# Feed-forwards of a two-block network: two tiles of each later set as plain products instead of seven products of summed quarters

## The chip, the cores and the metric

The kernel runs on one core of one Trainium2 chip, as a single program. The metric is device time in microseconds of one execution. Before the change the median of three runs is 1578.16 us, between 1577.29 and 1581.78 us.

## The reference, cut to what matters

All is float32, with 512 tokens and a model width of 1024. A first network has two layers: a pooling mixer and a feed-forward, then latent attention and a feed-forward. A second network of one layer follows, with differential attention and a mixture of experts. Only the two feed-forwards of the first network are touched by the change:

```python
def swiglu(h, w_gate, w_up, w_down):
    return (jax.nn.silu(h @ w_gate) * (h @ w_up)) @ w_down

h = rms_norm(x, norm_ffn[i])
x = x + swiglu(h, ffn_w_gate[i], ffn_w_up[i], ffn_w_down[i])
```

The gate and the up matrix are 1024 by 2816 each, the down matrix is 2816 by 1024.

## The kernel before, in words

**Three matmuls for one product.** TensorE multiplies in a float32 form that drops low bits, so each operand is split into a high and a low part: ScalarE (ACT) writes the high part as a rounded copy, and VectorE (DVE) or GpSimd (POOL) subtracts it from the original to get the low part. A product is then three matmuls: high by high, high by low, low by high (`mm3`). The weights come from memory in float32, so all of them are split while the kernel runs.

**Tiles and sets.** The hidden width of 2816 is cut into 22 tiles of 128 columns. `SETS` makes three sets of 8, 7 and 7 tiles. For each set the kernel first computes its gate and up tiles one by one (`ffn`, the loop over `j`), and then the set's share of the down product, for 8 blocks of 128 outputs (the loop over `d`), which is added to `x`. One tile's gate and up weights are one chunk of 128 by 2048, 1024 KB.

**Plain tile.** `plain` (tiles 0 to 4) and `later` (tile 5, on the normed x that `mixed_x` leaves in `full`) multiply a whole chunk: gate and up, each over 8 pieces of the width, 3 matmuls each, so 48 matmuls of 512 columns in two PSUM banks. `later` then does one silu, one product with the up bank and the split of the hidden tile (`hidden`). The chunk is split in four parts of 512 columns by `split_part`: four copies by ACT, two subtractions by DVE and two by POOL (`POOLED`).

**Mixed tile.** `mixed` (tiles 6 to 21) takes the chunk as a 2 by 2 grid of quarters (gate and up, by even and odd pieces of the width) and x as a 2 by 2 grid (even and odd pieces, by halves of the tokens), and forms the four result quarters from seven products of summed quarters instead of eight. That is 7 x 4 x 3 = 84 matmuls of 256 columns, in four PSUM banks. The sums of the weight quarters, their splits and the sums of the products are extra elementwise work: `split_mixed` is a list of eight steps (0 to 7), which leaves a first group of weights for products 0 to 3 (ready with step 5) and a second for products 4 to 6 (steps 6 and 7: one ACT copy of 1536 columns, then one DVE subtraction of 1536). Counted in the code, a mixed tile has 15 DVE instructions and a `later` tile 4.

**What sets the order.** The order of all instructions is written out by the program. `Stream.pump` takes the weight stream one step on and is called at fixed places: after each of the 7 products of a mixed tile and once more, and 16 times in `later`. The stream holds 2 raw chunks and 3 pairs of split chunks (`BUFS`). A plain chunk takes one pair, a mixed chunk two. `room` refuses a step while no pair is free; a pair is given back by `release` behind its last product. A raw buffer is loaded anew when its chunk's last step has been issued. `extra` holds table work for the layer that follows (for layer 0 the rotation tables, DVE and ACT work): one step behind product 3 and one behind product 6 of each mixed tile. All elementwise instructions are issued by one helper, so the profile puts them on one line, L445, and they are told apart by their tiles: `raw`, `hi`, `lo` are the weights, `bh`, `bl` the parts of x, `t`, `u` the result quarters, `hh`, `hl` the hidden tile, `rs` the sum of two weight quarters.

Of the kernel before, what the change touches and what calls it, by code (L numbers as in the profile page):

```python
# [22 lines left out]
FF = 2816  # L23
FT = FF // P

SETS = ((0, 8), (8, 15), (15, 22))
PLAIN = 6
H = T // 2


# [532 lines left out]
class Net:  # L563
# [296 lines left out]
    def mixed_x(self, l, full, parts):  # L860
# [3 lines left out]
        dve = nc.vector  # L864
        a, b = slice(0, H), slice(H, T)

# [43 lines left out]
    def ffn(self, l, hooks, after, extra=None):  # L910
# [13 lines left out]
        def go(n=1):  # L924

            for _ in range(n):
                if tail and next(tail[0], True):
                    tail.pop(0)

        def rest():  # L930
            while tail:
                go()

        def hidden(t):
            hh.append(self.tmp("hh", F32R))
            hl.append(self.tmp("hl", F32R))
            h, r = hh[-1], hl[-1]
            nc.scalar.activation(h, t, AF.Copy)
            yield
            nc.vector.tensor_tensor(r, t, h.bitcast(F32), op=OP.subtract)  # L940
# [10 lines left out]
        def plain(j):  # L951
            wh, wl = self.ws.take()
            pp = []

            def mm(m, k, begin, end):
                o = (2 * m + k % 2) * T + k // 2 * P
                c = slice(o, o + P)
                self.mm3(pp[m], wh[:, c], wl[:, c], xh[k], xl[k], begin, end)

            if j == PLAIN - 2:  # L960
                pp += [self.acc(), self.acc()]
                for k in range(KT):
                    for m in range(2):
                        mm(m, k, k == 0, k == KT - 1)
                    xh[k] = xl[k] = None
                    if k < 2:
                        go()
                    if k > 1:
                        next(mix, None)
                    if k == 4:  # L970
                        self.ws.pump(4)
            else:
                for m in range(2):
                    pp.append(self.acc())
                    for n, k in enumerate((0, 2, 4, 6, 1, 3, 5, 7)):
                        mm(m, k, n == 0, n == KT - 1)
                        if n in (0, 2):
                            go()
                        if not hooks and n in (1, 3, 6):
                            next(mix, None)  # L980
                    self.ws.pump(3)
                    if hooks:
                        hooks.pop(0)()
            self.ws.release()
            pend.append(pp)
            if not hooks:
                while pend:
                    tail.append(evac(*pend.pop(0)))
                    go()

        def later():
            wh, wl = self.ws.take()
            pp = []
            for m in range(2):
                ps = self.acc()
                for n, k in enumerate((0, 2, 4, 6, 1, 3, 5, 7)):
                    o = (2 * m + k % 2) * T + k // 2 * P
                    c = slice(o, o + P)
                    self.mm3(ps, wh[:, c], wl[:, c], *full[k], n == 0, n == KT - 1)
                    go()  # L1000
                    self.ws.pump()
                pp.append(ps)
            self.ws.release()
            t = self.tmp("t")
            nc.scalar.activation(t, pp[0], AF.Silu)
            nc.vector.tensor_tensor(t, t, pp[1], op=OP.mult)
            tail.append(hidden(t))
            go()

        def mixed():  # L1010
            g, s = self.tmp("t"), self.tmp("u")
            g0, g1, s0, s1 = g[:, :H], g[:, H:], s[:, :H], s[:, H:]
            got = None

            def product(n, out):
                nonlocal got
                if n in (0, 4):
                    got = self.ws.take_group(n == 4)
                c = (n % 4) * T
                for i, (bh, bl) in enumerate(parts[n]):  # L1020
                    k = slice(c + i * P, c + (i + 1) * P)
                    self.mm3(out, got[0][:, k], got[1][:, k], bh, bl, i == 0, i == KT // 2 - 1)
                if n in (3, 6):
                    self.ws.release()
                    if extra:
                        next(extra, None)
                go()
                self.ws.pump()

            def add(dst, x, y):  # L1030
                nc.vector.tensor_tensor(dst, x, y, op=OP.add)

            bank = []
            for n in range(7):
                if n % 2 == 0:
                    ps = self.acc()
                    bank += [ps[:, :H], ps[:, H:]]
                product(n, bank[n])
                if n == 1:
                    nc.scalar.activation(s1, bank[0], AF.Copy)  # L1040
                    add(g0, s1, bank[1])
                elif n == 3:
                    add(s0, s1, bank[2])
                    add(g1, s0, bank[3])
                    self.ws.pump()
                elif n == 5:
                    add(s1, g1, bank[5])
                    add(g1, g1, bank[4])
                    add(s0, s0, bank[5])
                    nc.scalar.activation(g, g, AF.Silu)  # L1050
            add(s0, s0, bank[6])
            nc.vector.tensor_tensor(g, g, s, op=OP.mult)
            tail.append(hidden(g))
            go()

        for f0, f1 in SETS:
            hh.clear()
            hl.clear()
            for j in range(f0, f1):
                if j < PLAIN - 1:  # L1060
                    plain(j)
                elif j < PLAIN:
                    for _ in mix:
                        pass
                    later()
                else:
                    mixed()
            rest()
            for d in range(KT):
                wh, wl = self.ws.take()  # L1070
                ps = self.acc()
                n = f1 - f0
                for f in range(n):
                    c = slice(f * P, (f + 1) * P)
                    self.mm3(ps, wh[:, c], wl[:, c], hh[f], hl[f], f == 0, f == n - 1)
                    if f % 3 == 1:
                        self.ws.pump()
                self.ws.flush()
                self.ws.release()
                nc.vector.tensor_tensor(self.x[:, d], ps, self.x[:, d], op=OP.add)  # L1080
                if f1 == FT:
                    after(d)

    def plain(self, j):
        return j < PLAIN

    def ffn_weights(self, l, arena=0):
        for f0, f1 in SETS:
            for j in range(f0, f1):
                self.ws.add(self.a["ffn_gu"][l, j], j < arena, not self.plain(j))  # L1090
            for d in range(KT):
                self.ws.add(self.a["ffn_dn"][l, d, :, f0 * P:f1 * P])
# [1409 lines left out]
```

## Time and profile before

| | us |
|---|---|
| median of three runs | 1578.16 |
| the profiled execution, its own time | 1573.54 |
| span of that execution, first to last instruction | 1571.7 |
| TensorE (PE) busy | 1494.9 |
| VectorE (DVE) busy | 1142.3 |
| ScalarE (ACT) busy | 827.7 |
| GpSimd (POOL) busy | 409.8 |

The span is what the trace shows of the profiled execution; 1.8 us of its time lie around it. PE counts as busy while any of its overlapping matmuls runs, so a matmul's own duration is longer than its share of the time: what it costs in a stream is read from the distance of two starts. A PE wait appears as idle time before the matmul that waited, with the engine that ended it. "PEclk" is the granted TensorE clock as a share of full speed.

### The profile page before, as it was taken

Reading aid. Unit: us, or ns where it says so; the run is one execution under the profiler, and the core shown is the slowest. Engines: PE = TensorE matmul, PEld = TensorE weight load, DVE = VectorE, ACT = ScalarE, POOL = GpSimd, SP = SyncE. Lnnn points to the kernel's source line nnn. Section 1 sums busy time; section 2 is a strip of 40 time slices with the busy share of each in tenths; the row PEclk is TensorE's granted clock in tenths of the full one; section 3 lists DMA queues with packets and bytes.
Section 4 is the critical chain, followed back from the end, with each engine's and each line's share of the span. In section 5 each row is a group of like instructions: output and inputs, shape, how many; then the busy total and the mean of one; then the engine's idle time right before and its main releaser. Section 6 shows DMA issues by size and latency. Waiting matters only on the chain.

```text
span 1571.7 us, 24066 instructions
## 1 busy us (share of the span) xinstructions
PE 1494.9 (95%) x8849; PEld 1263.2 (80%) x8849; DVE 1142.3 (73%) x2036; ACT 827.7 (53%) x1617; POOL 409.8 (26%) x330
## 2 busy tenths in 40 slices
PE   8999989989999999999999999999979799999997
PEld 7888878888878887888889889999978666666664
DVE  6794786686577756955965876898887487878774
ACT  5442343334455644433433444777785277777774
POOL 3323221231341112232222223223212223222221
PEclk9999999999999999999999999999989899999999
DMA  6114223323411103142222223121128799999982
GB/s 213 72 57 125 77 81 95 108 81 85 142 63 46 50 1 134 63 139 85 104 83 96 104 80 122 55 81 54 68 72 302 242 306 354 367 361 372 368 306 31
DMA packets 72250, 221.76 MB, mean 141 GB/s; under 512 B 7873, under 2 KB 17217, under 8 KB 58945
## 3 DMA queue, kind: packets, MB, share of 16 engines
q1 hardware_dynamic: 58752, 201.03, 36.8%
q0 software_dynamic: 4064, 14.16, 3.9%
q10 hardware_dynamic: 9312, 5.01, 1.1%
q8 instruction: 70, 1.15, 0.3%
q14 instruction: 52, 0.42, 0.1%
HBM read 208.63 MB, written 11.53 MB: 140 GB/s over the span
## 4 chain that ended last, share of the span: by engine, by line
PE 66%; DVE 18%; ACT 7%; issue 5%; DMA 3%; POOL 1%; ACTq 0%; DVEq 0%; POOLq 0%; SPq 0%
PE acc L445 54%; PE pss L445 8%; DVE lo L445 5%; PE pst L445 4%; DVE t L445 4%; ACT hi L445 3%; DVE u L445 2%; DVE raw L445 2%; DVE p L445 1%; DVE bl L445 1%; DMA raw<-ffn_gu 1%; DVE x L445 1%; DVE xl L445 1%; ACT p L445 1%; DMA bnd<-bands 0%
## 5 line engine op out<-in xcount | busy, mean ns | idle before, releaser
L445 ACT ACTIVATE hi<-raw 128x512 fp32r<-128x512 f32 (+3 forms) x346 | 242.8, 728 | 233.3 <-DVE raw L445 107.6
L445 PE MATMUL acc<-bh,lo 128*128 128x256 f32 (+1 forms) x928 | 271.4, 292 | 23.5 <-DVE lo L445 23.5
L445 DVE TENSOR_TENSOR lo<-raw,hi 128x512 fp32r<-128x512 f32 (+2 forms) x237 | 254.2, 1074 | 37.2 <-ACT hi L445 37.1
L445 PE MATMUL acc<-bh,hi 128*128 128x256 f32 (+1 forms) x928 | 269.7, 291 | 3.4 <-ACT hi L445 3.4
L445 PE MATMUL acc<-bl,hi 128*128 128x256 f32 (+1 forms) x928 | 268.6, 289 | 0.0
L445 POOL TENSOR_TENSOR lo<-raw,hi 128x512 fp32r<-128x512 f32 (+2 forms) x109 | 142.5, 1309 | 474.7 <-ACT hi L445 408.7
L445 DVE TENSOR_TENSOR wl<-raw,wh 128x512 fp32r<-128x512 f32 x288 | 202.6, 747 | 53.0 <-ACT wh L445 43.0
L445 PEld LDWEIGHTS acc<-bh,lo 128*128 128x128 f32 x928 | 180.7, 195 | 30.0 <-DVE lo L445 28.8
L445 PEld LDWEIGHTS acc<-bh,hi 128*128 128x128 f32 x928 | 180.6, 195 | 6.7 <-ACT hi L445 5.2
L445 PEld LDWEIGHTS acc<-bl,hi 128*128 128x128 f32 x928 | 180.8, 195 | 1.6
L445 ACT ACTIVATE wh<-raw 128x512 fp32r<-128x512 f32 x320 | 177.4, 620 | 0.0
L445 DVE TENSOR_TENSOR x<-acc,x 128x512 f32<-128x512 f32 x75 | 51.4, 688 | 121.6 <-PE acc L445 121.5
L445 PE MATMUL acc<-hl,hi 128*128 128x512 f32 x352 | 137.5, 391 | 0.2 <-DVE hl L445 0.2
L445 PE MATMUL acc<-hh,hi 128*128 128x512 f32 x352 | 137.2, 390 | 0.3 <-ACT hh L445 0.3
L445 PE MATMUL acc<-hh,lo 128*128 128x512 f32 x352 | 137.0, 389 | 0.0
L445 PE MATMUL acc<-hi,xh 128*128 128x256 f32 x384 | 111.0, 289 | 0.0
L445 PE MATMUL acc<-lo,xh 128*128 128x256 f32 x384 | 108.7, 283 | 0.6 <-DVE lo L445 0.6
L445 PE MATMUL acc<-hi,xl 128*128 128x256 f32 x384 | 108.5, 283 | 0.0
L445 PE MATMUL acc<-wh,teh 128*96 128x512 f32 x224 | 103.1, 460 | 0.0
L445 POOL TENSOR_TENSOR rs<-raw 128x512 f32<-128x512 f32 x32 | 45.2, 1412 | 218.7 <-DVE u L445 74.0
L445 PE MATMUL acc<-wl,teh 128*96 128x512 f32 x224 | 88.1, 393 | 0.8 <-DVE wl L445 0.8
L445 PE MATMUL acc<-wh,tel 128*96 128x512 f32 x224 | 88.5, 395 | 0.0
(349 smaller groups left out, 3446.5 us busy)
## 6 DMA issues: line engine op xcount, KB each, us to landing
raw<-moe_w SPq DMA_DIRECT2D x200, 256.0 KB
raw<-moe_w SPq DMA_DIRECT2D x46, 1024.0 KB
raw<-ffn_gu SPq DMA_DIRECT2D x43, 1024.0 KB
raw<-ffn_dn SPq DMA_DIRECT2D x32, 448.0 KB
raw<-da_in SPq DMA_DIRECT2D x12, 1024.0 KB
raw<-ffn_dn SPq DMA_DIRECT2D x16, 512.0 KB
raw<-mla_up SPq DMA_DIRECT2D x4, 832.0 KB
raw<-mla_o_a SPq DMA_DIRECT2D x12, 256.0 KB
```

Of the source, the lines that this page charges most:

```text
L445: r = f(*args, **kw)
```

## The change

`plain` also answers yes for the second and the fifth tile (offsets 1 and 4) of the second and the third set, in both layers. These tiles (9, 12, 16 and 19) are no longer marked as mixed in the weight stream, and the loop calls `later` for them. A set of seven then runs M P M M P M M (M mixed, P plain), and 12 of 22 tiles are mixed instead of 16.

```diff
+BETWEEN = (1, 4)
...
                     for _ in mix:
                         pass
                     later()
+                elif self.plain(j):
+                    later()
                 else:
                     mixed()
...
     def plain(self, j):
-        return j < PLAIN
+        return j < PLAIN or any(f0 and j - f0 in BETWEEN for f0, f1 in SETS if f0 <= j < f1)
```

In the list of instructions, eight tiles change in all (two layers, two sets, two tiles): 36 matmuls, 11 DVE instructions and 1 ACT instruction fewer for each. The order of every engine is the same outside these four stretches, and so is the order of the loads.

The first place is ACT in the third set of layer 0, where the second group of a mixed tile that follows another mixed tile is copied. Before, for the set's second tile (the first two rows are the silu and the hidden copy of the tile ahead):

```order
L445 ACTIVATE t<-t 128x512
L445 ACTIVATE hh<-t 128x512
L445 ACTIVATE hi<-raw 128x1536
L445 ACTIVATE u<-acc 128x256
L445 ACTIVATE hi<-raw 128x1024
L445 ACTIVATE hi<-rs 128x512
```

Now, for the set's fourth tile, which follows the third (the last row but two is the third tile's silu):

```order
L447 ACTIVATE hi<-rs 128x512
L447 ACTIVATE hi<-raw 128x512
L447 ACTIVATE hi<-raw 128x1536
L447 ACTIVATE t<-t 128x512
L447 ACTIVATE hh<-t 128x512
L447 ACTIVATE hi<-raw 128x512 x2
```

The copy of 1536 columns has moved ahead of the silu and the hidden copy of the tile before it; the rows of 512 behind are parts of the next, plain chunk.

The second place is DVE at the same two tiles. Before:

```order
L445 TENSOR_TENSOR u<-u,acc 128x256
L445 TENSOR_TENSOR t<-t,u 128x512
L445 TENSOR_TENSOR hl<-t,hh 128x512
L445 TENSOR_TENSOR lo<-raw,hi 128x1536
L445 TENSOR_TENSOR t<-u,acc 128x256
L445 TENSOR_TENSOR lo<-raw,hi 128x1024
```

Now:

```order
L447 TENSOR_TENSOR u<-t,acc 128x256
L447 TENSOR_TENSOR t<-t,acc 128x256
L447 TENSOR_TENSOR u<-u,acc 128x256
L447 TENSOR_TENSOR lo<-raw,hi 128x1536
L447 TENSOR_TENSOR u<-u,acc 128x256
L447 TENSOR_TENSOR t<-t,u 128x512
L447 TENSOR_TENSOR hl<-t,hh 128x512
L447 TENSOR_TENSOR lo<-raw,hi 128x512
```

The subtraction of 1536 columns stood behind the whole tail of the tile ahead (last sum, product with silu, split of the hidden tile); now it stands in front of that tail.

## Rows read from the trace of the kernel before

**Rows 1.** The page: span, PE and DVE, and the chain that ended last.

```profile
span 1571.7 us, 24066 instructions
...
PE 1494.9 (95%) x8849; PEld 1263.2 (80%) x8849; DVE 1142.3 (73%) x2036; ACT 827.7 (53%) x1617; POOL 409.8 (26%) x330
...
PE 66%; DVE 18%; ACT 7%; issue 5%; DMA 3%; POOL 1%; ACTq 0%; DVEq 0%; POOLq 0%; SPq 0%
```

**Rows 2.** Busy time by stretch: gate and up of sets 2, 3, both layers.

```profile
core 0: us, PE busy (x) PEld busy (x) DVE busy (x) ACT busy (x) POOL busy (x), PEclk, DMA share, GB/s
169.18:253.77 84.59, 75.14 (x590) 72.70 (x588) 71.50 (x106) 33.23 (x49) 15.84 (x11) 0.98 0.23 77
292.09:372.49 80.40, 74.08 (x590) 72.46 (x588) 67.41 (x99) 33.56 (x48) 16.54 (x11) 0.98 0.24 81
728.60:808.18 79.58, 73.83 (x589) 72.40 (x588) 66.69 (x97) 32.38 (x47) 16.49 (x11) 0.98 0.25 83
846.29:925.81 79.52, 74.10 (x590) 72.48 (x588) 67.32 (x99) 33.71 (x48) 16.88 (x11) 0.98 0.24 81
sum 324.09, PE 297.16 PEld 290.04 DVE 272.92 ACT 132.88 POOL 65.74; mean PE 74.29 PEld 72.51 DVE 68.23 ACT 33.22 POOL 16.44
```

**Rows 3.** Start and duration on PE: a plain tile's end, a mixed tile's start.

```profile
105.03 0.39 PE L445 MATMUL acc<-bl,hi 128*128 128x512 f32 x1
105.26 0.39 PE L445 MATMUL acc<-bh,lo 128*128 128x512 f32 x1
105.48 0.28 PE L445 MATMUL acc<-bh,hi 128*128 128x256 f32 x1
105.60 0.28 PE L445 MATMUL acc<-bl,hi 128*128 128x256 f32 x1
```

**Rows 4.** Busy time by stretch, set 1: plain tile 5, mixed 6, 7; both layers.

```profile
94.60:105.48 10.88, 10.88 (x49) 9.01 (x48) 10.35 (x16) 3.96 (x7) 2.49 (x4) 1.00 0.08 26
105.48:125.64 20.16, 20.16 (x170) 20.15 (x169) 17.65 (x29) 9.41 (x16) 2.64 (x2) 1.00 0.27 79
652.84:663.76 10.92, 10.92 (x50) 8.96 (x49) 10.37 (x17) 5.06 (x9) 1.39 (x2) 1.00 0.09 24
663.76:683.91 20.15, 20.15 (x170) 20.15 (x168) 16.05 (x28) 9.62 (x15) 5.50 (x15) 1.00 0.36 110
```

**Rows 5.** PE by form, third set, layer 0: busy, mean ns, idle before, releaser.

```profile
L445 PE MATMUL acc<-bh,lo 128*128 128x256 f32 x196 | 56.7, 289 | 5.4 <-DVE lo L445 5.4
```

**Rows 6.** Busy time by stretch: inside the second set of layer 0.

```profile
226.48:229.89 3.41, 3.41 (x17) 3.41 (x17) 3.38 (x7) 0.82 (x2) 0.00 (x0) 0.50 0.77 262
```

**Rows 7.** In order of time, third set of layer 0, second tile: ACT.

```profile
305.45 0.63 ACT L445 ACTIVATE hh<-t 128x512 fp32r<-128x512 f32 x1 [2.97 <-DVE t L445]
305.99 1.47 ACT L445 ACTIVATE hi<-raw 128x1536 fp32r<-128x1536 f32 x1
```

**Rows 8.** The same tile: DVE, then PE.

```profile
304.15 1.27 DVE L445 TENSOR_TENSOR t<-t,u 128x512 f32<-128x512 f32 x1
307.49 1.76 DVE L445 TENSOR_TENSOR lo<-raw,hi 128x1536 fp32r<-128x1536 f32 x1 [0.68 <-ACT hi L445]
...
309.31 0.39 PE L445 MATMUL acc<-bh,lo 128*128 128x256 f32 x1 [0.98 <-DVE lo L445]
```

**Rows 9.** DVE by form, 94.60 to 125.64: a plain tile's DVE work.

```profile
L445 DVE TENSOR_TENSOR lo<-raw,hi 128x512 fp32r<-128x512 f32 x4 | 3.3, 834 | 0.0
L445 DVE TENSOR_TENSOR hl<-t,hh 128x512 fp32r<-128x512 f32 x3 | 2.1, 693 | 1.5 <-ACT hh L445 1.5
L445 DVE TENSOR_TENSOR t<-t,acc 128x512 f32<-128x512 f32 x1 | 0.7, 681 | 0.0
```

**Rows 10.** In order of time, set 1 of layer 0, tile 7's second group: DVE.

```profile
116.32 1.75 DVE L445 TENSOR_TENSOR lo<-raw,hi 128x1536 fp32r<-128x1536 f32 x1
```

**Rows 11.** DVE by form, second set of layer 0: a step of the tables.

```profile
L445 DVE SCALAR_TENSOR_TENSOR ang<-k,ang 128x512 f32<-128x512 f32 x4 | 3.2, 808 | 0.0
```

**Rows 12.** Who waited for whom, third set of layer 0: total, times, longest.

```profile
POOL rs L445 <- DMA raw<-ffn_gu: 9.5, 1, 9.5
```

## The prediction

> **What bounds the kernel now.** I read the page first, then the busy times of the stretches that the change touches, then single instructions in them. The page says that PE is busy for 1494.9 us of 1571.7, that most of the chain that ended last is PE's (66%), and that DVE has the next share (18%) [rows 1]. So two things can shorten the kernel: fewer or cheaper matmuls, or fewer waits of PE for DVE. The change makes the matmuls dearer, so all depends on the waits.
>
> The four touched stretches are the gate and up products of sets 2 and 3 in both layers. They take 84.59, 80.40, 79.58 and 79.52 us, together 324.09 [rows 2]. What they would take without a wait follows from the distance of two starts: a matmul of 256 columns follows another after 0.12 us (105.48 to 105.60), one of 512 after 0.22 to 0.23 (105.03, 105.26, 105.48) [rows 3]. A mixed tile has 84 of the first kind: 84 x 0.12 = 10.08 us. The two mixed tiles of set 1 take just that: 20.16 and 20.15 us, with PE busy throughout [rows 4]. Seven tiles should then take 70.56, and four stretches 4 x 70.56 = 282.2. The difference, 324.1 - 282.2 = **41.9 us**, is lost to waiting, 1.5 us for each of 28 mixed tiles.
>
> Where it goes: PE's idle time in the four stretches is 324.09 - 297.16 = 26.9 us [rows 2]. In the third set of layer 0 nearly all of it, 5.4 us, is ended by DVE writing `lo` [rows 5]. The granted clock is 0.98 in each stretch [rows 2], where it is 1.00 in set 1 [rows 4]; in one piece of 3.41 us after a series of waits it is 0.50, the 1.2 GHz level [rows 6]. Half of such a piece is lost, 1.7 us, so four of them make about 6.8. The remaining 8 us are the slow restarts: the matmul behind a wait takes 0.39 us instead of 0.28 [rows 3, 8], and the next one starts late.
>
> Why DVE is late: one wait followed back. In the third set's second tile, DVE's product with silu runs from 304.15 to 305.42 [rows 8], ACT's hidden copy follows to 306.08, and only behind it stands the copy of 1536 columns, from 305.99 to 307.46 [rows 7]. Then DVE subtracts, 307.49 to 309.25, and PE, which waited 0.98 us for this, starts at 309.31 [rows 8]. So the second group of a tile's weights is made behind the tail of the tile before it. DVE has no time to catch up: it is busy 67.41 us for seven tiles, 9.6 us a tile, against PE's 10.08, and in the second set of layer 0, which carries the table steps, 71.50, 10.2 us a tile [rows 2].
>
> **The change part by part.** *Matmuls.* In each stretch two mixed tiles go, 2 x 10.08 us of PE time, and two plain ones come. A plain tile took 10.88 and 10.92 us in set 1, with PE busy throughout [rows 4]; I take 10.90. Each swap costs 10.90 - 10.08 = 0.82 us on the path, eight cost **+6.6 us**. This part is certain, since PE runs it in any case.
>
> On this price a rule speaks more strongly against the change. By the Trainium skill, TensorE: Matmul & The Clock Gate, section "Wait — 56ns, not 53.3ns?", back-to-back matmuls start N / 2.4 GHz plus about 2.5 ns apart at the full clock, which an estimate makes 109 ns for 256 columns and 216 for 512. By it a swap would cost 48 x 0.216 - 84 x 0.109 = 1.2 us, eight 9.7, and the forecast would be 3 us later. The trace does not agree: it shows 120 ns and 227 (10.90 / 48), so the short matmuls carry more of the fixed cost here than the page has.
>
> *Elementwise work.* A mixed tile's 15 DVE instructions become 4. The four cost 2 x 0.834 for `lo`, 0.681 for the product with the up bank and 0.693 for `hl`, in sum 3.0 us [rows 9]. A stretch then asks DVE for 5 x 9.6 + 2 x 3.0 = 54 us while PE runs 5 x 10.08 + 2 x 10.90 = 72.2. In the second set of layer 0 ten table steps fall into the stretch; at 0.808 us [rows 11] they bring it to 62. In the third set of layer 0 DVE's share goes from 67.41 of 80.40 (84%) to 75%; in the second it is 86% of a stretch without waits. ACT and POOL were busy at most 33.71 and 16.88 us of some 80 [rows 2] and stay far below. That work lies beside PE and costs nothing as long as it comes in time, which the order decides:
>
> *Order.* `later` calls the stream 16 times and needs only two PSUM banks and one pair of split chunks. The mixed chunk behind a plain tile is finished during it, and the stream comes a full tile ahead. The eight steps of the mixed tile after that then fit into the eight calls of the first one, so that its copy and its subtraction of 1536 columns now stand ahead of the first tile's tail and no longer behind it; the two listings of the change show this on ACT and DVE. Whether this is early enough is shown by set 1, where the same three tiles P M M already run in this order. There tile 7's subtraction of 1536 columns ends at 116.32 + 1.75 = 118.07 [rows 10]. Tile 7 starts at 105.48 + 10.08 = 115.56 and needs it for its fifth product, 48 matmuls later, at 121.3: 3.2 us to spare. In the second set of layer 0 two table steps of 0.8 us lie ahead instead of a shorter one, so at least 1.6 us are left.
>
> *Waits that stay.* The trace has no set M P M M P M M, so I bound them. Below, nothing: set 1 has no PE idle time in P M M in either layer [rows 4]. Above, each of the 20 mixed tiles left keeps its 1.5 us: 20 x 1.5 = 29.9. I take zero, since set 1 has the same code in the same order; the first tile of a set, which follows the down products, has no wait now either (in the third set of layer 0 the first is the second tile's at 309.31 [rows 8]).
>
> *Edits at no cost.* The order of the loads is unchanged. A mixed chunk behind a plain one is loaded when the tile before that has emptied its buffer; POOL once waited 9.5 us for a load [rows 12]. The plain tile's 10.9 us cover it. The last table step of layer 0 moves into the third set; 0.8 us of DVE, hidden. The down products and all else keep their order.
>
> **Sum.** 20 x 10.08 + 8 x 10.90 = 201.6 + 87.2 = 288.8 us instead of 324.1: **35.3 us less**. The profiled execution would go from 1573.54 to 1538.2. That execution was 4.6 us faster than the median of the runs shown, 1578.16; against the median the forecast is **1542.9 us**.
>
> **The rivals.** *The second mixed tile of each pair still waits.* It has no plain tile ahead of it, its first group gets its pair only when the plain tile ends, and DVE has 9.6 us of work in its 10.08. Eight such tiles at 1.5 us keep 12 us: 1542.9 + 12.0 = 1554.9. Against it stands the margin of 3.2 us in set 1.
>
> *Waits per mixed tile stay as they are*, because they come from the tile's own chain of ACT, DVE and PSUM and not from lack of DVE time: 29.9 us stay, 5.4 are gained, 1572.8. For it: the wait is ended by DVE at moments when DVE itself has waited, 0.68 us for ACT [rows 8]. Against it: set 1 has the same chain without a wait.
>
> *Slower: the load comes too late at a plain tile.* With two raw buffers the chunk behind a plain tile cannot be loaded before the mixed tile ahead has used its own; ACT's first copy of it stands in the queue ahead of that tile's silu, so a late load would hold back ACT, then DVE, then PE. If the whole 9.5 us of the one such wait [rows 12] reached PE at each of eight plain tiles, that would be 76 us: 1542.9 + 76.0 = 1618.9. It decides from 35.3 / 8 = 4.4 us a tile on. Against it: the wait ended inside a tile's time and fell on POOL, and a whole plain tile lies between the load and its use.
>
> That the change does not do what it says is excluded by the listing of instructions.
>
> **How the numbers follow.** The forecast gets 0.72, the rival of the pair 0.14, unchanged waits 0.08, the late load 0.03; 0.03 is left for a result near the old time for a reason I do not see. A measurement of this kernel can tell about 0.3% from no change, 4.7 us. Forecast, pair and most of the unchanged waits (1572.8 is 5.4 below) are faster by more: 0.92. Within 0.3%: 0.05. Slower: 0.03. The range takes in the forecast and the pair rival. Its low end is 4.6 us under the forecast, as the profiled execution was under its median: 1538. Its high end is the pair rival plus 3.6 us, the distance of the slowest run shown from the median: 1559.
>
> **What would show it.** Right: the four stretches at 72 to 73 us each with PE idle near zero, plain tiles of 10.9, granted clock 1.00, DVE below 65 us in each. The pair rival would show idle time ended by `lo` in the fourth and the seventh tile of each set and nowhere else. The late load would show ACT waiting for `raw` from memory and PE waiting in the tile behind. A saving that appears outside the four stretches, or waits for `lo` right after a plain tile, would make the reasoning wrong even if the time came out.

## Result and profile after

The changed kernel takes 1539.39 us, median of four runs (1534.21 to 1539.75), against 1577.72 for the kernel before in the same comparison: a ratio of 0.9746, 95% interval 0.9718 to 0.9774. The traced execution took 1539.18 us. Two later comparisons gave medians of 1537.99 (ratio 0.975, interval 0.9725 to 0.9774) and 1542.22 (0.9763, interval 0.9740 to 0.9786).

The page of the changed kernel, which answers to [rows 1]:

```profile
span 1537.4 us, 23426 instructions
...
PE 1487.6 (97%) x8561; PEld 1250.4 (81%) x8561; DVE 1088.1 (71%) x1948; ACT 815.8 (53%) x1609; POOL 414.0 (27%) x330
...
PE 82%; DVE 7%; ACT 5%; DMA 2%; issue 1%; POOL 1%; ACTq 0%; POOLq 0%; SPq 0%; DVEq 0%
```

PE's part of the chain rose from 66% to 82%, DVE's fell from 18% to 7%. Busy times by stretch, for the same four stretches as [rows 2]:

```profile
168.87:241.06 72.19, 72.19 (x517) 68.40 (x516) 58.23 (x86) 30.54 (x47) 21.06 (x14) 1.00 0.29 94
279.17:351.36 72.19, 72.19 (x517) 68.40 (x516) 57.17 (x81) 31.16 (x47) 21.16 (x14) 1.00 0.29 94
706.60:778.79 72.19, 72.19 (x518) 68.40 (x516) 54.05 (x78) 30.03 (x46) 20.41 (x14) 1.00 0.29 94
816.90:889.09 72.19, 72.19 (x518) 68.40 (x516) 55.63 (x80) 31.26 (x47) 21.83 (x14) 1.00 0.28 94
sum 288.76, PE 288.76 PEld 273.60 DVE 225.08 ACT 123.00 POOL 84.45; mean PE 72.19 PEld 68.40 DVE 56.27 ACT 30.75 POOL 21.11
```

PE is busy for all of the 72.19 us, four times over, and the granted clock is 1.00 instead of 0.98. The sum went from 324.09 to 288.76. One of the new plain tiles, the second tile of the first of these stretches:

```profile
178.94:189.85 10.91, 10.91 (x50) 9.02 (x49) 9.07 (x10) 4.06 (x6) 4.17 (x3) 1.00 0.19 81
```

In the third set of layer 0 the matmuls that had waited 5.4 us for `lo` [rows 5] wait no more (PE by form, idle time behind the second bar):

```profile
L447 PE MATMUL acc<-bh,lo 128*128 128x256 f32 x140 | 39.6, 283 | 0.0
```

And in order of time on DVE, the subtraction of 1536 columns for that set's fourth tile, which answers to [rows 10]:

```profile
310.11 1.75 DVE L447 TENSOR_TENSOR lo<-raw,hi 128x1536 fp32r<-128x1536 f32 x1
```

The third tile starts at 279.17 + 10.08 + 10.90 = 300.15, the fourth 10.08 us later at 310.23, and its fifth product, which needs this, is due 48 matmuls (5.76 us) later, at 316.0. It is ready at 311.86, 4.1 us early.

### The profile page after: what moved, and what is told of

Read it like the earlier page. It is cut to its first block, busy times and chain, and to the rows that moved or that the text cites. A ratio compares the mean times of both kernels' runs of the same rounds, so it can differ in the third digit from the quotient of the medians.

```text
span 1537.4 us, 23426 instructions
## 1 busy us (share of the span) xinstructions
PE 1487.6 (97%) x8561; PEld 1250.4 (81%) x8561; DVE 1088.1 (71%) x1948; ACT 815.8 (53%) x1609; POOL 414.0 (27%) x330
## 4 chain that ended last, share of the span: by engine, by line
PE 82%; DVE 7%; ACT 5%; DMA 2%; issue 1%; POOL 1%; ACTq 0%; POOLq 0%; SPq 0%; DVEq 0%
PE acc L447 70%; PE pss L447 8%; PE pst L447 4%; DVE lo L447 1%; DVE bl L447 1%; ACT hi L447 1%; ACT p L447 1%; DMA raw<-ffn_gu 1%; DVE xl L447 1%; DMA bnd<-bands 1%; DVE t L447 1%; DVE p L447 1%; DVE x L447 0%; DMA out<-ring,idx 0%; DVE xe L447 0%
## 5 line engine op out<-in xcount | busy, mean ns | idle before, releaser
L447 ACT ACTIVATE hi<-raw 128x512 fp32r<-128x512 f32 (+3 forms) x354 | 235.7, 697 | 211.2 <-PE acc L447 95.8
L447 POOL TENSOR_TENSOR lo<-raw,hi 128x512 fp32r<-128x512 f32 (+2 forms) x125 | 167.0, 1340 | 629.7 <-ACT hi L447 600.4
L447 PE MATMUL acc<-bl,hi 128*128 128x256 f32 (+1 forms) x832 | 252.5, 304 | 0.0
L447 PE MATMUL acc<-bh,hi 128*128 128x256 f32 (+1 forms) x832 | 252.5, 303 | 0.0
L447 PE MATMUL acc<-bh,lo 128*128 128x256 f32 (+1 forms) x832 | 252.4, 303 | 0.0
L447 DVE TENSOR_TENSOR lo<-raw,hi 128x512 fp32r<-128x512 f32 (+2 forms) x229 | 230.9, 1010 | 28.5 <-ACT hi L447 28.0
L447 PEld LDWEIGHTS acc<-bl,hi 128*128 128x128 f32 x832 | 159.0, 191 | 6.6
L447 PEld LDWEIGHTS acc<-bh,hi 128*128 128x128 f32 x832 | 159.0, 191 | 6.6
L447 PEld LDWEIGHTS acc<-bh,lo 128*128 128x128 f32 x832 | 159.0, 191 | 6.3
L447 PE MATMUL acc<-xh,hi 128*128 128x512 f32 x200 | 79.8, 399 | 1.2 <-ACT xh L447 1.2
```

Source lines behind the costliest of these rows:

```text
L447: r = f(*args, **kw)
```

## Experiments

What is open is why the waits are gone: because the order put the second weight group ahead of the previous tile's tail, or because DVE has less to do. Each diff is against the changed kernel unless it says otherwise.

**The order without the relief.** No plain tile in between; at the end of the down products the stream is taken as far ahead as it goes:

```diff
-BETWEEN = (1, 4)
+BETWEEN = ()
...
                     if f % 3 == 1:
                         self.ws.pump()
+                if d >= 6 and f1 < FT:
+                    self.ws.pump(8)
                 self.ws.flush()
```

> No plain tile at offsets 1 and 4 (16 of 22 tiles mixed, as before), but the weight stream is taken as far ahead as its buffers allow at the end of the down products of sets 1 and 2, so that in sets 2 and 3 each copy and subtraction of 1536 columns stands ahead of the tail of the tile before it. Theory of the order (PE waited because the second weight group was made behind the previous tile's tail; DVE itself, 9.6 us a tile against 10.08, can keep up): the four stretches take 7 x 10.08 = 70.6 us each, 282 in sum, no waits for lo, and the kernel takes 1539.4 - 6.6 = 1533 us. Theory of the load on DVE (PE waited because DVE has too much work in a mixed tile, and the 88 instructions fewer removed the waits): the first two tiles go through, then the waits come back at up to 1.5 us a tile, stretches of 77 to 80 us, 1560 to 1572 us.

Measured: 1556.37 us, ratio 0.9855 (0.9830 to 0.9880). The four stretches:

```profile
169.28:247.31 78.03, 74.67 (x590) 72.62 (x589) 69.92 (x105) 33.39 (x49) 17.28 (x11) 0.98 0.23 80
286.36:359.77 73.41, 71.44 (x589) 70.80 (x588) 64.80 (x97) 32.77 (x47) 17.04 (x11) 1.00 0.25 85
716.01:788.95 72.94, 71.47 (x589) 70.81 (x588) 64.44 (x95) 32.07 (x45) 17.89 (x11) 1.00 0.25 85
828.71:902.99 74.28, 71.46 (x590) 70.81 (x589) 65.58 (x96) 31.94 (x45) 16.62 (x11) 1.00 0.25 84
sum 298.66, PE 289.04 PEld 285.04 DVE 264.73 ACT 130.17 POOL 68.83; mean PE 72.26 PEld 71.26 DVE 66.18 ACT 32.54 POOL 17.21
```

The lead is worth 25 us of the 41.9 (324.09 - 298.66), but not all. In the third set of layer 0 no wait comes for 44 us, then one of 0.73 us and one of 1.23; the second set of layer 0 waits from 34 us on. DVE falls behind, tile by tile. Its timeline in the fifth and the sixth tile of that third set:

```profile
331.67 1.75 DVE L447 TENSOR_TENSOR lo<-raw,hi 128x1536 fp32r<-128x1536 f32 x1
...
335.25 0.69 DVE L447 TENSOR_TENSOR hl<-t,hh 128x512 fp32r<-128x512 f32 x1 [0.70 <-ACT hh L447]
336.19 1.23 DVE L447 TENSOR_TENSOR lo<-raw,hi 128x1024 fp32r<-128x1024 f32 x1 [0.26 <-ACT hi L447]
...
339.66 1.00 DVE L447 TENSOR_TENSOR raw<-raw 128x512 f32<-128x512 f32 x1
340.58 1.76 DVE L447 TENSOR_TENSOR lo<-raw,hi 128x512 fp32r<-128x512 f32 x1
...
343.38 1.75 DVE L447 TENSOR_TENSOR lo<-raw,hi 128x1536 fp32r<-128x1536 f32 x1
```

And POOL's at the time of two slow instructions, those at 339.66 and 340.58:

```profile
338.52 1.59 POOL L447 TENSOR_TENSOR rs<-raw 128x512 f32<-128x512 f32 x1 [8.44 <-DMA raw<-ffn_gu]
340.19 1.61 POOL L447 TENSOR_TENSOR raw<-raw 128x512 f32<-128x512 f32 x1
```

From one subtraction of 1536 columns to the next DVE needs 343.38 - 331.67 = 11.71 us, PE 10.08. DVE is idle for only 0.96 of it, both times for ACT. Two instructions that take 0.68 us in the run without POOL's sums below take 1.00 and 1.76 while POOL works. The two waits of PE in this set:

```profile
330.69 0.39 PE L447 MATMUL acc<-bh,lo 128*128 128x256 f32 x1 [0.73 <-DVE lo L447]
342.40 0.39 PE L447 MATMUL acc<-bh,lo 128*128 128x256 f32 x1 [1.23 <-DVE lo L447]
```

The second is ended by the slow subtraction of 512 columns itself (340.58 + 1.76 = 342.34), the first by the same instruction one tile earlier, and not by the subtraction of 1536. So DVE's load is the deeper bound, and the order only puts off the moment when it shows.

**The relief without the order.** The plain tiles stay, but take the stream only four steps on, so that the subtraction of 1536 columns stands behind the tail of the tile before it again:

```diff
                     go()
-                    self.ws.pump()
+                    if j == PLAIN - 1 or n % 4 == 3:
+                        self.ws.pump()
                 pp.append(ps)
```

> The changed kernel with its plain tiles at offsets 1 and 4, but they take the weight stream only 4 steps on instead of up to 16, so that the next tiles' copy and subtraction of 1536 columns stand behind the tail of the tile before them, as before the change. DVE has the same work as in the changed kernel. Theory of the order: waits for lo come back at the fifth product of the mixed tiles at offsets 2, 3, 5 and 6, about 1.4 us each, some 5.6 us a stretch: 77 to 78 us, about 1561 us. Theory of the load on DVE: no waits, 72.2 us a stretch, 1539 us.

Measured: 1544.56 us in one run, and in the four stretches:

```profile
168.97:242.52 73.55, 72.70 (x518) 68.51 (x516) 57.51 (x83) 29.44 (x46) 19.83 (x13) 1.00 0.26 89
280.85:353.04 72.19, 72.19 (x518) 68.40 (x516) 55.88 (x77) 29.45 (x44) 20.70 (x13) 1.00 0.27 92
708.81:781.00 72.19, 72.19 (x517) 68.39 (x516) 53.27 (x75) 29.26 (x45) 20.03 (x13) 1.00 0.28 91
819.14:891.33 72.19, 72.19 (x517) 68.40 (x516) 54.93 (x77) 30.50 (x46) 21.50 (x14) 1.00 0.27 92
```

The theory that the new order is needed falls: with the old order three stretches have no wait, and the one with the table steps loses 1.4 us. The rest of this one execution's distance from the changed kernel lies mostly behind 929 us, where it takes 613.36 us at a granted clock of 0.96; the change does nothing there. It is close, though. In the third set of layer 0:

```profile
314.30 0.69 DVE L447 TENSOR_TENSOR hl<-t,hh 128x512 fp32r<-128x512 f32 x1 [0.70 <-ACT hh L447]
315.67 1.76 DVE L447 TENSOR_TENSOR lo<-raw,hi 128x1536 fp32r<-128x1536 f32 x1 [0.68 <-ACT hi L447]
```

The fourth tile starts at 280.85 + 2 x 10.08 + 10.90 = 311.9 and needs this at 317.7; it is there at 317.43, 0.2 us early, against 4.1 in the changed kernel. With the plain tiles in place, what the order adds is margin.

**One plain tile instead of two.**

```diff
-BETWEEN = (1, 4)
+BETWEEN = (1,)
```

> One plain tile a set instead of two, the second (offset 1): M P M M M M M. Theory of the order: the stream is a tile ahead behind the plain tile and stays there, no waits, 6 x 10.08 + 10.90 = 71.4 us a stretch, 285.5 in sum, 1536 us. Theory of the load on DVE: no waits up to the fourth tile, then 1.5 us in each of the last three or four, 76 to 77 us a stretch, about 1558 us.

Measured: 1545.66 us, ratio 0.9803 (0.9777 to 0.9829). Sum of the four stretches, and then the four groups of down products behind them:

```profile
sum 288.65, PE 287.06 PEld 278.28 DVE 247.23 ACT 127.93 POOL 81.13; mean PE 71.76 PEld 69.57 DVE 61.81 ACT 31.98 POOL 20.28
...
sum 155.94, PE 154.38 PEld 125.87 DVE 81.30 ACT 59.24 POOL 42.65; mean PE 38.60 PEld 31.47 DVE 20.32 ACT 14.81 POOL 10.66
```

Both theories had it half. Three stretches have no wait at 71.4 us; the one with the table steps has 1.6 us in its sixth tile and takes 74.5. But five mixed tiles in a row leave work behind: the down products take 155.9 us, 39.0 each, where the changed kernel's take 38.1 each; PE's waits at their start are for the last hidden tile (`hh` from ACT, `hl` from DVE). The traces account for 3.4 us against the changed kernel (444.6 us for both parts, against 441.2); the medians of the same comparison lie 7.7 apart, and the rest is not accounted for.

**The shared path.** From the run with the lead and no plain tiles, the two sums on POOL are left out:

```diff
-            self.both = self.net.tmp("rs")
-            pool.tensor_tensor(self.both, r, s, op=OP.add)
+            self.both = r
...
             lo(0, 2, pq)
-            pool.tensor_tensor(r, p, r, op=OP.subtract)
```

> The run with the lead and without plain tiles, with the two sums of weight quarters that POOL forms for each mixed tile left out (the up matrix's even quarter stands in their place). DVE's instructions are the same in number and size. Theory of the shared path (DVE instructions that read two SBUF tiles take 1.0 to 1.8 us instead of 0.69 while POOL runs): they go back to 0.69, DVE's cycle falls from 11.7 to 10.3 us a tile, waits nearly vanish, 70.6 to 71.5 us a stretch. Theory of DVE's own load and its turns with ACT: the cycle stays above 11 us, 73 to 74 us a stretch.

Measured: 1538.78 us in one run. Sum of the four stretches:

```profile
sum 283.03, PE 282.82 PEld 282.40 DVE 241.03 ACT 132.41 POOL 7.91; mean PE 70.70 PEld 70.60 DVE 60.26 ACT 33.10 POOL 1.98
```

DVE's timeline in the third set of layer 0:

```profile
320.54 1.76 DVE L445 TENSOR_TENSOR lo<-raw,hi 128x1536 fp32r<-128x1536 f32 x1
...
328.53 0.68 DVE L445 TENSOR_TENSOR raw<-raw 128x512 f32<-128x512 f32 x1
329.13 0.68 DVE L445 TENSOR_TENSOR lo<-raw,hi 128x512 fp32r<-128x512 f32 x1
...
330.85 1.76 DVE L445 TENSOR_TENSOR lo<-raw,hi 128x1536 fp32r<-128x1536 f32 x1
```

As many DVE instructions of the same sizes, seven mixed tiles a stretch, and the waits are gone but for 0.2 us. The two instructions are back at 0.68, and the cycle is 330.85 - 320.54 = 10.31 us. The difference of 1.40 to the 11.71 is just what the two had grown by: (1.00 - 0.68) + (1.76 - 0.68). A rival would be that the engines had waited for the results of POOL's sums, which this run leaves out too; but in the run with the sums no engine has a wait in the four stretches that POOL ends.

**More work for POOL.** From the run with the lead and no plain tiles, one of DVE's subtractions goes to POOL:

```diff
             dve.tensor_tensor(p, self.both, p, op=OP.subtract)
-            lo(3, 1, self.both)
+            c = slice(3 * self.PART, 4 * self.PART)
+            pool.tensor_tensor(self.group[1][:, c], self.both, self.group[0][:, c].bitcast(F32),
+                               op=OP.subtract)
```

> The run with the lead and without plain tiles, with one of DVE's subtractions of 512 columns per mixed tile (the low part of the sum of two quarters, 0.69 us) done by POOL, which is busy a fifth of the time. Theory of DVE's own load: DVE's cycle falls from 11.7 to 11.0 us, waits fall by 0.7 us a tile, about 71 to 72 us a stretch. Theory of the shared path: POOL's new 1.3 to 1.6 us slow other DVE instructions by as much as was saved; 73 to 75 us a stretch, no gain.

Measured: 1558.39 us in one run; sum of the four stretches:

```profile
sum 301.95, PE 290.79 PEld 286.48 DVE 265.09 ACT 130.54 POOL 106.64; mean PE 72.70 PEld 71.62 DVE 66.27 ACT 32.63 POOL 26.66
```

301.95 against 298.66, and DVE busy 265.09 against 264.73 with one instruction a tile fewer: DVE got nothing from it, as the theory of the shared path says.

**Both helps at once.** The lead at the start of a set, and one plain tile in the middle (`BETWEEN = (3,)` with the extra `pump(8)` from above):

> The lead at the start of a set from the run without plain tiles, and one plain tile in the middle of each set (offset 3): M M M P M M M. DVE falls behind by some 1.6 us a mixed tile (11.7 against 10.08) and the lead covered three tiles; the plain tile should give it back before the fourth. Expected: no waits in three stretches, 6 x 10.08 + 10.90 = 71.4 us each, 72 to 74 in the second set of layer 0 with its table steps, down products of 38.1 to 38.5 us, and a kernel 1 to 3 us faster than the changed one: 1535 to 1537 us. Rival: three mixed tiles at the end of a set leave work behind that delays the down products, 39 us or more each as in the run with one plain tile, and the kernel is 2 to 5 us slower than the changed one.

> One plain tile in the middle and the lead, again, beside the changed kernel on the same chip: its four stretches are 3.3 us shorter in sum (285.5 against 288.8). If only they count, it is 3 us faster, 1535 to 1537 us, and the ratio to the kernel before is lower by 0.002. If its medians are again not below the changed kernel's, the gain is lost in the parts behind 1100 us, where the time at half speed differs.

Measured: 1540.07 us, ratio 0.9745 (0.9720 to 0.9769), and the second time 1541.81, ratio 0.9769 (0.9749 to 0.9789), beside the changed kernel's 1542.22 on the same chip. No stretch has a wait:

```profile
sum 285.51, PE 285.51 PEld 277.91 DVE 240.32 ACT 126.59 POOL 71.12; mean PE 71.38 PEld 69.48 DVE 60.08 ACT 31.65 POOL 17.78
```

The stretches of the first traced execution are 3.3 us shorter than the changed kernel's, as reckoned, but the difference of the whole (0.4 us in the one shared comparison) cannot be told from none.

**The spread of executions.** Both kernels were traced again unchanged:

> The kernel before once more, for a second trace of it. If the profiled execution on which the sum was made is a fast one of its kind because it had fewer pieces at the lower clock, this one (likely near 1579 us) has the four stretches at about the same 324 us but more time at half speed, a few us of it in the stretches where PE waits or behind them. If instead the waits themselves vary, the sum of the four stretches is several us above 324.

> The changed kernel once more, for the spread of its executions. If the distance between the forecast (1542.9 against the median, 1538.2 against the profiled execution) and the measurement comes from executions that differ and not from the change, the four stretches take 72.2 us each again, while the time of the whole varies by some 5 us with the granted clock in the experts' part behind 927 us; executions between 1534 and 1541 us. If the change saved more than reckoned, some stretch outside the four is shorter in every execution.

> The kernel before, a third trace. If the profiled execution on which the forecast was made was a favourable one outside the four stretches, this one again has 324 to 325 us in them and more time at half speed behind 1100 us than that one's 33 us, in a total of 1575 to 1582 us. If the stretches themselves vary by 4 us or more from execution to execution, the forecast's 324.1 us was an unlucky base.

> The changed kernel, a third trace, timed beside lead_middle_2 on the same chip. Four stretches of 72.2 us, 1537 to 1540 us. Its executions differ only behind the feed-forwards.

> The kernel before, a fourth trace, for the same question as before_third.

The part from the start of the differential attention to the end, in the execution before on which the forecast rests (busy time by stretch):

```profile
964.07:1571.69 607.62, 573.24 (x3376) 448.22 (x3374) 465.10 (x982) 411.53 (x893) 158.31 (x128) 0.97 0.65 219
```

In the second and the third trace of the kernel before it takes 610.35 and 611.09 us, in the fourth:

```profile
963.15:1575.41 612.26, 576.98 (x3376) 451.73 (x3374) 465.79 (x982) 411.08 (x893) 158.06 (x128) 0.96 0.64 218
```

In the three traces of the changed kernel it takes 610.19, 608.61 and 614.26 us; the second of them is this row:

```profile
926.63:1535.24 608.61, 573.37 (x3376) 449.10 (x3374) 466.35 (x982) 411.15 (x893) 158.09 (x128) 0.97 0.65 219
```

The same instructions take 607.6 to 612.3 us before and 608.6 to 614.3 after, longer where the granted clock is lower: of these seven, 0.97 in the two shortest (607.62 and 608.61) and 0.96 in the five others. The change did nothing there. The four stretches vary little: 324.09, 324.89, 324.71 and 325.24 us before, and in each trace of the changed kernel that was summed 288.76.

## Why the prediction was right, and where it was not

**The sum held.** 20 x 10.08 + 8 x 10.90 = 288.8 us was forecast for the four stretches, 288.76 was measured; 1538.2 us was forecast for the traced execution, 1539.18 was measured. The price of the swap, 6.6 us, follows from the same rows, and the distance of 0.227 us for 512 columns held: plain tiles take 10.9. That the whole came out within 1 us of the 1538.2 is partly luck, since traced executions of the changed kernel took 1537.07 to 1542.22 us; the 288.8 is not, since every trace that was summed has it. The bound of zero for the waits that stay was the true one. The half-speed pieces in the four stretches went with the waits, as the clock of 1.00 shows.

**The step that failed is the carry to the median:** "That execution was 4.6 us faster than the median of the runs shown, 1578.16; against the median the forecast is 1542.9". It took a distance between two executions of the old kernel for one that the new kernel would have as well, and then set the low end of the range, 1538, by that same distance. The new kernel has no such distance: its traced execution took 1539.18 us and its median is 1539.39. The ratio of 0.9746 makes 1537.6 us of the old median in the same comparison (1577.72) and 1538.1 of 1578.16, 5 us below the 1542.9 and on or just under the low end; its interval reaches down to 1533.7.

The later traces show what the 4.6 us were. Part was work of the change: from the start of the second set to the end of the third set's down products, in both layers, the execution that the forecast used took

```profile
169.18:410.92 241.74, 225.97 (x1514) 208.10 (x1513) 177.53 (x261) 94.63 (x146) 56.69 (x42) 0.99 0.28 92
728.60:964.07 235.47, 224.30 (x1514) 207.84 (x1512) 175.91 (x258) 97.88 (x151) 57.02 (x42) 0.99 0.29 95
```

together 477.2 us, the other three 479.2, 479.5 and 478.0. The changed kernel takes 441.2:

```profile
168.87:389.47 220.60, 220.60 (x1369) 199.88 (x1368) 150.13 (x217) 88.90 (x142) 61.87 (x44) 1.00 0.31 101
706.60:927.20 220.60, 220.60 (x1370) 199.88 (x1368) 148.01 (x214) 92.24 (x147) 61.22 (x44) 1.00 0.30 101
```

So 36.0 us are saved against that execution and 36.8 to 38.3 against the others, 37.3 on average: the 35.3 was 2 us too small. Of the 37.3, 36.0 are in the four stretches, and 1.3 are in the down products, a term that the prediction put at nothing ("The down products and all else keep their order") and whose place outside the stretches it had named as a sign against its reasoning. In the old kernel they took 152.7 to 154.8 us, now 152.4; in the two slowest cases PE waited 0.9 and 1.1 us in them for the last hidden tile. The rest of the 4.6 us was chance in a part that the change does not touch: 607.62 us against 610.4 to 612.3. Averaged over all traces, everything outside the touched part took 1096.5 us both before and after. The savings by medians, 41, 38 and 35 us, scatter about the traces' 37.3.

**The reason given for the waits was too narrow.** The prediction said that the order decides whether the work comes in time. With the old order and the relief, three of four stretches have no wait; with the new order and no relief, all four do. The order alone takes out 25 of the 41.9 us, the relief alone all but 1.4, and with the relief the order turns a margin of 0.2 us into 4.1. So the relief of DVE is enough almost by itself, and the order is not. The bound from set 1 was right, but for both reasons at once, since there too a plain tile stands ahead.

**A term was mis-sized:** "it is busy 67.41 us for seven tiles, 9.6 us a tile, against PE's 10.08". That is an average over a stretch whose first tile is prepared before it begins and whose last prepares only down chunks. In the middle of a set, in the run with the lead, a mixed tile costs DVE a cycle of 11.71 us: 10.31 as it is without POOL's sums, and 1.40 from sharing with them. By 9.6 DVE could keep up, and seven mixed tiles with a lead should run without waits; they do not. In the changed kernel's third set of layer 0 DVE is busy for 57.17 us, where the prediction had 54. The forecast was saved by the plain tiles' slack, 10.9 us of PE time against 3.0 of DVE work, which is enough with the larger figure too. In the old kernel the sharing was there to be read: ahead of the wait that the prediction followed back the product with silu took 1.27 us [rows 8], and a subtraction of 512 columns stands just ahead of it in that trace:

```profile
302.07 1.65 DVE L445 TENSOR_TENSOR lo<-raw,hi 128x512 fp32r<-128x512 f32 x1
```

POOL ran beside both, from 301.88 to 304.87:

```profile
301.88 1.29 POOL L445 TENSOR_TENSOR rs<-raw 128x512 f32<-128x512 f32 x1 [14.09 <-DVE t L445]
303.24 1.63 POOL L445 TENSOR_TENSOR raw<-raw 128x512 f32<-128x512 f32 x1
```

At 0.69 each the two DVE instructions would have ended 1.5 us earlier, about the delay of that second group, 309.25 against the 307.9 at which it was due. That it alone made this wait is reckoned, not tried.

**The rivals.** The second tile of a pair did not wait. The unchanged waits did not stay. The late load showed itself, but only to ACT and POOL, which in the third set of layer 0 waited 3.2 and 2.5 us for `raw` from memory; PE has no idle time in any plain tile or behind one.

## What to carry to other kernels

Before paying matmul columns to save matmul columns, price both sides in the engine that prepares the operands: here seven products instead of eight saved 0.8 us of TensorE a tile and cost VectorE a cycle of 11.7 us against 10.1. A cheap tile between costly ones lets the preparing engine catch up: here two in seven were enough, and one in seven where the stream started ahead. Look also at what runs behind the stretch, where a backlog comes out. And make a forecast against one trace's own time, but set its range by the spread of executions, which a second trace of the same kernel would show.

## What was not expected of the hardware

VectorE instructions that read two SBUF tiles grew from 0.68 us to 1.00 and 1.76 us while GpSimd ran a two-input instruction, and the GpSimd one mostly grew too, from 1.29 us to some 1.6. With the GpSimd sums left out both VectorE instructions went back. Moving a VectorE instruction to the idle-looking GpSimd gained nothing (301.95 us against 298.66).

In the traces two things go with whether a VectorE instruction grows. One is what it reads: those that take one input from PSUM (`acc`) did not grow. In the run with four stream steps, GpSimd works from 317.03 to 320.29, and between two subtractions that grew stand two PSUM readers at their usual length:

```profile
317.03 3.26 POOL L447 TENSOR_TENSOR lo<-raw,hi 128x512 fp32r<-128x512 f32 x2 [18.83 <-ACT hi L447]
...
317.68 1.46 DVE L447 TENSOR_TENSOR lo<-raw,hi 128x512 fp32r<-128x512 f32 x1
319.06 0.41 DVE L447 TENSOR_TENSOR u<-u,acc 128x256 f32<-128x256 f32 x1
319.50 0.42 DVE L447 TENSOR_TENSOR t<-u,acc 128x256 f32<-128x256 f32 x1
319.84 1.00 DVE L447 TENSOR_TENSOR lo<-raw,hi 128x512 fp32r<-128x512 f32 x1
```

The other is which started first. Counted over the whole trace of the kernel before, for VectorE and GpSimd instructions on two tensors, the VectorE ones of 128 by 512: with two SBUF inputs, none of the 87 that began ahead of the GpSimd one beside them took more than 0.70 us, and of the 120 that began while a GpSimd one had more than 0.3 us left to run 114 took more than 0.75, up to 1.80. With one input in PSUM, none of the 52 beside GpSimd took more than 0.70.

The Trainium skill has the sharing in the GPSIMD Engine Reference, section 1, Specifications: GpSimd's SBUF interfaces are shared with VectorE, which contends when its instruction has two SBUF inputs. The trace agrees, with the numbers above. That the sharing decided the waits in the run with the lead is shown by the run without the sums.
